# A hybrid decoder layer on one core: weights of the first projections by contraction block, and four edits to a planned order

## The chip, the cores and the metric

The kernel runs on one core of a Trainium2 chip. Its engines work side by side, each through its own list of instructions: TensorE (PE, with PEld for its weight loads), VectorE (DVE), ScalarE (ACT), GpSimd (POOL) and SyncE (SP), which issues nearly all transfers. The metric is the device time in microseconds (us) of one execution. Before the change the median of three runs is 917.85 us (917.58 to 918.46).

## The reference

One inference step of one layer, all in float32: a prompt of 512 tokens and 8 sequences of 4 new tokens each (544 tokens together, 1024 features).

```python
shift, scale, gate = jnp.split(jax.nn.silu(c) @ w_cond + b_cond, 3, axis=-1)
h = x * (1 + scale[:, None]) + shift[:, None]
qa, ka, va, za, qkv_b, zb, a_b, b_b, ga, gb = split_columns(h @ w_in)
# branch A: dilated sliding-window softmax attention, windows 128, 512, 2048, 8 heads x 64 each,
#           the three outputs combined by softmax-denominator share, times silu(za)
# branch B: conv of width 4 + silu on q/k/v, l2-normed q/k, chunked gated delta rule (8 heads x 128):
u = solve_unit_lower(I + strict(beta * k k^T * decay), [beta * v, beta * k * exp(cum)])
merged = sigmoid(ga) * (yA @ w_branch_a) + sigmoid(gb) * (yB @ w_branch_b)
y = LayerNorm(ALPHA * x + gate * (merged @ w_out))
```

(The line with `solve_unit_lower` stands for the triangular solve of each chunk of the delta rule.) It returns `y` for both kinds of tokens, the new key and value caches, and the states of branch B.

## The kernel before, in words

**Exact products in three passes.** TensorE multiplies float32 rounded to a shorter format (float32r) in one pass. Where full precision is wanted the kernel splits both operands into a rounded part and a rest (`hi`/`lo` of a weight, `hhi`/`hlo` of the activations) and sums `hhi*hi`, `hhi*lo` and `hlo*hi`. ACT makes `hi`, and DVE `lo`. Products in plain float32 (attention, delta rule) show as two records per matmul in the trace.

**The front.** `c` (`cT`, nine conditioning vectors, padded to 32 columns) is loaded on ACT's queue and gives `cs`, its silu. SP loads, in this order, eight 1 MB blocks `wm` of the conditioning weights; among them the constants `cst`, the activations `xT` in four loads of two blocks, and the first three weight tiles (128x1024, 512 KB each, into the three `wraw` buffers). For each of the eight contraction blocks k: eight matmuls make `pd` from `wm[k]` and `cs`; ACT copies it to `Y`; two small matmuls `pd<-cst,Y` turn it into scale and shift; DVE modulates `xT[k]`; ACT and DVE split it into `hhi`/`hlo`; and the first three projections (q, k and v of head 0 of branch B, jobs 0 to 2) take their three passes over block k. The weights of the first two are split in halves (`whi`, `wlo`, 128x512) and that of the third whole (`hi`, `lo`). They accumulate in the tiles `pp`, `pg` and `pb`. Fillers (`warm`) are put into TensorE's list where the planner expects it idle.

**The stream.** Some 90 more weight tiles (`wt<-in_w_in`) follow through the same three buffers, loaded by SP up to five jobs ahead and split up to two jobs ahead. Beside them run generators ("threads", each with a rank): the gates of branch B (`pg<-cg,abT` is the product that ends them), the inverses of the delta rule's chunks (`delta_blocks`, one thread for the eight heads, rank 1), the rule itself (rank 0), the attention of prompt and samples. In `delta_blocks` small blocks go through memory and back (`dtz` and `Tc`, `drows` and `cr`).

**The attention's probability products.** `prompt_attention` makes, for each of 4 head pairs and 4 query blocks, two transposed tiles `PT` of probabilities and then six or eight 128x64 by 128x128 matmuls `pg<-PT,vrow`, 120 in all.

**The end.** After the branches are merged (`mhi`, `mlo`, and `ms` for the sample rows), the last product runs over two halves of `w_out`: `wo0h`/`wo0l`, and then `wo1h`/`wo1l`. `load_out(n)` loads and splits a half in four pieces; DVE makes `r` and `lo` of an accumulator `pp` with the gate (`gs` of the samples, `gp` of the prompt), which frees it.

**The planner.** No engine's order is written by hand. Each call is recorded, and `schedule()` then places all instructions with a model of their costs: an instruction becomes a candidate once its inputs and a buffer are there by the model, and the candidate of the lowest rank and oldest number goes first on its engine. Calls inside `rec.together()` are placed without anything between them. `ENTER` is the model's cost of going over to another tile shape on TensorE, `op.extra` what a transfer takes beside its bytes until its reader may start, and `LINES` names the kinds of buffers that are given out per thread. The model only sets the order; on the chip each engine waits for what it needs. All instructions are emitted by one line, so in the profile every row of this kernel has L721 (after the change L722).

Of the kernel before, what the change touches and what calls it, by code (L numbers as in the profile page):

```python
# [259 lines left out]
class Recorder:  # L260
# [5 lines left out]
    AGAIN = {"pe": 0.0, "ve": 0.11, "se": 0.14, "ge": 0.11, "sp": 0.0}  # L266
    HOLD = 1.0
    GAP, HEAT, FULL = 0.25, 3.0, 17.0
    ENTER = {(128, 128): 0.197, (64, 128): 0.197, (64, 64): 0.142, (32, 32): 0.073, (128, 64): 0.1, (128, 32): 0.0,
             (64, 32): 0.1, (32, 128): 0.2, (32, 64): 0.1}  # L270
    ENGINES = ("pe", "ve", "se", "ge", "sp")
    FREE = ("g", "d", "b")

    def __init__(self):
        self.ops, self.events, self.rank, self.now, self.idle = [], [], 0, 0.0, 0.0
# [87 lines left out]
    def cost(self, op, args):  # L363
# [35 lines left out]
        elif e == "se":  # L399
            c = (0.155 if in_psum else 0.21) + 0.83e-3 * n  # L400
            a = (0.07 if "accum_out" in op.kw else 0.0) + (0.08 if pointer else 0.0)
            ix = op.outs[0].ix
            if n > 16 and ix.ndim > 1 and abs(int(ix.flat[1]) - int(ix.flat[0])) > 4:
                a += 1.0e-3 * n
            op.cost, op.late = c - 0.1 + a, 0.1
            f = args[2]
            op.table = None if f in (AF.Copy, AF.Square, AF.Abs) else "sqrt" if f == AF.Sqrt else "exp"
        elif e == "ge":
            c = {"memset": 0.08 + 0.85e-3 * n, "tensor_copy": 0.21 + 0.8e-3 * n,
                 "tensor_scalar": 0.25 + 2.45e-3 * n}.get(op.name, 0.25 + 2.05e-3 * n)  # L410
            op.cost, op.late = c - 0.05, 0.05
        else:
            runs, total = [], 0
            for v in (args[0], args[1]):
                r = 1
                if isinstance(v, View):
                    at = v.ix
                    steps = [(int(np.take(at, 1, axis=d).flat[0]) - int(at.flat[0]), k) if k > 1 else (0, 1)
                             for d, k in enumerate(at.shape)]
                    if v.base.pool.side != "dram":  # L420
                        steps = steps[1:]
                else:
                    steps = [(int(a), int(b)) for a, b in v.ap]
                for st, k in reversed(steps):
                    if k > 1 and st != r:
                        break
                    r *= k
                runs.append(min(r * 4, 32768))
            out = args[0]
            total = 4 * (out.ix.size if isinstance(out, View) else math.prod(b for _, b in out.ap))  # L430
            run = min(runs)
            dram = [not isinstance(v, View) or v.base.pool.side == "dram" for v in (args[0], args[1])]
            if not dram[0]:
                per, op.extra = run / (26e3 if self.front else 23.3e3), 1.75
                if isinstance(args[1], View):
                    op.extra += 1.0 if run >= 2048 else 2.3
            elif not dram[1]:
                per, op.extra = 0.026 + run / 60e3, 1.1
            else:
                per, op.extra = 0.044 + run / 21.7e3, 1.9  # L440
            if dram[0] and run < 512:
                op.extra += 0.5
            op.transfer = per * max(total / run / 16, 1)
            op.cost, op.late, op.table = 0.53 if dram[0] and dram[1] else 0.42, 0.0, None
            sbuf = [v for v in op.outs + op.ins if v.base.pool.side != "dram"]
            if sbuf and sbuf[0].shape[0] <= 32 and min(runs) < 2048:
                op.cost = 0.68


    def schedule(self):  # L450
# [9 lines left out]
        for op in ops:  # L460
# [6 lines left out]
            for t in op.tiles:  # L467
                if not hasattr(t, "left"):
                    t.left = 0
                    t.line = t.key + (op.part if t.kw.get("tag") in self.FREE else 0,)  # L470
                    tag.setdefault(t.key, []).append(t)
                    lines.setdefault(t.line, []).append(t)
                t.left += 1
# [300 lines left out]
def body(ctx, tc, io):  # L774
# [95 lines left out]
    ahead = {}  # L870
    with ExitStack() as fctx:
        fr = pool(fctx, "front", 1)
        cT = fr.tile([128, KT, 32], F32, name="cT")
        se.dma_start(cT, io["cT"])
        bT = fr.tile([128, 24], F32, name="bT")
        se.dma_start(bT, io["bT"])
        th = fr.tile([128, KT, 32], F32, name="th")
        se.activation(th, cT, AF.Tanh, scale=0.5)
        ve.tensor_scalar(th, th, 0.5, 0.5, op0=OP.mult, op1=OP.add)
        ve.tensor_mul(cs, cT, th)  # L880
        mb = fr.tile([128, KT, 2], F32, name="mb")
        ve.tensor_copy(mb[:, :, 0], bT[:, 0:8])
        ve.tensor_scalar(mb[:, :, 1], bT[:, 8:16], 1.0, None, op0=OP.add)
        xT = fr.tile([128, KT, NT], F32, name="xT")
        wm = [fr.tile([128, KT, 256], F32, name="wm", bufs=6) for _ in range(KT)]
        for k in range(KT):
            sp.dma_start(wm[k], io["w_mod"][k])
            if k == 0:
                sp.dma_start(cst, io["const"])
            if k % 2 == 0:  # L890
                sp.dma_start(xT[:, k:k + 2], io["xT"][:, k:k + 2])
            if k in FIRST:
                i = FIRST.index(k)
                raws[i] = wraw.tile([128, D], F32, name="wt", tag="wraw")
                sp.dma_start(raws[i], io["w_in"][TILE_AT["b", 0, (1, 0, 2)[i]]])
        rec.front = False
        sp.dma_start(wab, io["w_ab"])
        sp.dma_start(tables["g"], io["const_g"])
# [1 line left out]
        sp.dma_start(dta, io["dta"])  # L900

        for i in range(3):
            if i == 2:
                hi, lo = split(raws[i], D, ve)
                weights[i] = [(hi[:, 128 * k:128 * k + 128], lo[:, 128 * k:128 * k + 128]) for k in range(KT)]
                continue
            weights[i] = []
            for u in range(2):
                hi = op.tile([128, NT], F32R, name="whi", tag="o")[:, :512]
                lo = op.tile([128, NT], F32R, name="wlo", tag="o")[:, :512]  # L910
                raw = raws[i][:, 512 * u:512 * u + 512]
                se.activation(hi, raw, AF.Copy)
                ve.tensor_sub(lo, raw, hi.bitcast(F32))
                weights[i] += [(hi[:, 128 * k:128 * k + 128], lo[:, 128 * k:128 * k + 128]) for k in range(4)]
        ahead = {0: [pp(), pp()], 1: [pg(), pg()], 2: [pg(), pb_()]}
        mod = fr.tile([128, KT, 2, 9], F32, name="mod")
        xs = xT[:, :, SEQ:].rearrange("p k (b t) -> p k b t", t=4)
        for k in range(KT):
# [10 lines left out]
            pv = pc[:, 256:288].rearrange("p (a b) -> p a b", b=16)  # L929
            for u in range(2):  # L930
                pe.matmul(pv[:, u, 0:9], Y[:, 128 * u:128 * u + 128], C("selc"), start=True, stop=True)
            m = mod[:, k]
            ve.tensor_add(m, pv[:, :, 0:9], mb[:, k, :, None].to_broadcast([128, 2, 9]))
            per_token = lambda u: m[:, u, 1:9, None].to_broadcast([128, 8, 4])
            ve.tensor_mul(xs[:, k], xs[:, k], per_token(1))
            ve.tensor_add(xs[:, k], xs[:, k], per_token(0))
            h = xT[:, k]
            ve.tensor_scalar(h[:, :SEQ], h[:, :SEQ], m[:, 1, 0:1], m[:, 0, 0:1], op0=OP.mult, op1=OP.add)
# [522 lines left out]
    def prompt_attention():  # L1461

        for j in range(4):
# [55 lines left out]
            for i in range(4):  # L1519
# [12 lines left out]
                    PTs.append(PT)  # L1532
                    yield 1.2 + 0.5 * hh

                for c in range(c0_, 4):
                    for hh in range(2):
                        hp = slice(64 * hh, 64 * hh + 64)
                        g = max(c - 1, 0)
                        v = vrow[g][:, i - 1 if c == 0 else i, hp]
                        pe.matmul(pnv[hp, c > 1, i % 2, :], v, PTs[hh][:, c, :], start=c in (c0_, 2), stop=c in (1, 3))  # L1540
# [752 lines left out]
def lay_out(x):  # L2293
# [17 lines left out]
        "cT": np.pad(c.T.reshape(KT, 128, 9).transpose(1, 0, 2), ((0, 0), (0, 0), (0, 23))),  # L2311
# [18 lines left out]
        "ln_g": a["ln_g"],  # L2330
        "ln_b": a["ln_b"],
        "w_ab": w[:, OFF_AB:OFF_AB + 16].reshape(KT, 128, 16).transpose(1, 0, 2),
        "w_in": wt.reshape(len(TILES), KT, 128, 128).transpose(0, 2, 1, 3).reshape(len(TILES), 128, D),
    }
    return {k: np.ascontiguousarray(v) for k, v in d.items()}
# [34 lines left out]
```

## Time and profile before

| | |
|---|---|
| median of three runs | 917.85 us (917.58 to 918.46) |
| the profiled execution | 918.74 us |
| its span, first to last instruction | 917.0 us |
| mean granted clock of TensorE | 0.993 |
| TensorE busy | 893.8 us |
| DVE busy | 728.4 us |
| ACT busy | 430.3 us |
| moved by DMA | 239.50 MB, mean 261 GB/s |

Rows of the timeline read: start in us, duration in us, engine, line, operation, output<-inputs, shapes, count, and in brackets how long the engine had been idle and for what. A matmul's duration includes the way through the array, so matmuls that follow one another start closer together than they last, and the distance between starts is their price. Rows of groups show busy time and the mean of one in ns.

### The profile page before, as it was taken

The numbers are of one execution on the slowest core, as the hardware profiler recorded it, in microseconds if no ns is written. First come the engines' busy times: TensorE is split into PE (matmuls) and PEld (weight loads), VectorE is DVE, ScalarE is ACT, GpSimd is POOL, SyncE is SP. The second block draws the span as 40 slices with busy tenths as digits, with TensorE's granted clock in tenths as the row PEclk, the third lists the DMA queues.
The fourth block names the chain that finished last, engine by engine and source line by source line (L and its number), as shares of the span: only waits on it lengthen the run. The fifth ranks groups of instructions, "written<-read, shape, count | busy, mean of one in ns | idle before, by whom it ended". The sixth has DMA issues, their size and how long they took to land.

```text
span 917.0 us, 20414 instructions
## 1 busy us (share of the span) xinstructions
PE 893.8 (97%) x7874; PEld 835.8 (91%) x7874; DVE 728.4 (79%) x1637; ACT 430.3 (47%) x1007; POOL 77.4 (8%) x185
## 2 busy tenths in 40 slices
PE   8999999999999999999999999999999999999895
PEld 7899999899999999989899999999999999997684
DVE  3576757778568999989999987468879999867658
ACT  3375644867354675446657337524422222235311
POOL 0132011102000012001140000000110000000000
PEclk9999999999999999999999999999999999999998
DMA  9775777457758988989687785599899999988813
GB/s 372 287 196 196 223 215 237 143 174 239 231 171 274 301 278 281 297 260 333 214 299 238 255 258 161 173 298 378 261 335 362 324 398 418 335 308 299 266 41 118
DMA packets 108918, 239.50 MB, mean 261 GB/s; under 512 B 31554, under 2 KB 65484, under 8 KB 105108
## 3 DMA queue, kind: packets, MB, share of 16 engines
q1 hardware_dynamic: 108532, 238.04, 77.2%
q8 instruction: 62, 1.02, 0.5%
q14 instruction: 36, 0.29, 0.1%
q10 hardware_dynamic: 288, 0.14, 0.1%
HBM read 221.57 MB, written 104.26 MB: 355 GB/s over the span
## 4 chain that ended last, share of the span: by engine, by line
PE 79%; DVE 8%; DMA 6%; ACT 3%; SPq 1%; issue 1%; DVEq 0%; POOL 0%; ACTq 0%
PE pp L721 59%; PE pg L721 10%; PE pd L721 7%; PE pb L721 3%; DVE r L721 2%; DMA wm<-in_w_mod 2%; DVE acc L721 1%; SPq L721 1%; DMA rbo<-dO 1%; DMA wt<-in_w_in 1%; DVE lo L721 1%; DMA wv<-dw 1%; ACT L721 1%; DMA S<-in_state_delta 1%; DMA cT<-in_cT 1%
## 5 line engine op out<-in xcount | busy, mean ns | idle before, releaser
L721 PE MATMUL pp<-hhi,hi 128*128 128x272 f32 x1360 | 400.4, 294 | 2.7 <-DVE spare L721 1.8
L721 PE MATMUL pp<-hhi,lo 128*128 128x272 f32 x1360 | 400.6, 295 | 0.0
L721 PE MATMUL pp<-hlo,hi 128*128 128x272 f32 x1360 | 400.3, 294 | 0.0
L721 PEld LDWEIGHTS pp<-hhi,hi 128*128 128x128 f32 x1360 | 257.2, 189 | 5.4 <-DVE spare L721 2.1
L721 PEld LDWEIGHTS pp<-hlo,hi 128*128 128x128 f32 x1360 | 257.2, 189 | 2.9 <-issue 2.1
L721 PEld LDWEIGHTS pp<-hhi,lo 128*128 128x128 f32 x1360 | 256.8, 189 | 2.6 <-issue 1.6
L721 ACT ACTIVATE hi<-wt 128x1024 fp32r<-128x1024 f32 (+1 forms) x102 | 104.6, 1025 | 174.8 <-PE pp L721 141.5
L721 DVE TENSOR_TENSOR lo<-wt,hi 128x1024 fp32r<-128x1024 f32 (+1 forms) x102 | 120.1, 1177 | 40.6 <-ACT hi L721 40.1
L721 DVE SCALAR_TENSOR_TENSOR acc<-ext,cw,acc 128x568 f32<-128x568 f32 x72 | 57.4, 801 | 5.7 <-ACT acc L721 5.3
L721 ACT ACT_TABLE_LOAD x36 | 46.2, 1283 | 7.3 <-DVE acc L721 4.3
L721 DVE TENSOR_TENSOR slab<-slab 128x512 f32<-128x512 f32 (+1 forms) x66 | 43.0, 667 | 1.2 <-ACT slab L721 1.1
L721 DVE TENSOR_REDUCE slab<-slab 128x8 f32<-128x512 f32 (+2 forms) x66 | 43.0, 657 | 0.2
L721 POOL COPY cx<-ext 128x3 f32<-128x3 f32 (+1 forms) x48 | 33.9, 734 | 90.2 <-ACT ext L721 90.0
L721 ACT ACTIVATE zt<-pp 128x272 f32<-128x272 f32 x48 | 18.6, 388 | 45.8 <-PE pp L721 37.7
L721 ACT ACTIVATE P<-P,st 128x256 f32<-128x256 f32 (+1 forms) x64 | 31.2, 489 | 16.1 <-DVE st L721 15.7
L721 PE MATMUL pp<-ybl,hi 128*128 128x272 f32 x128 | 36.9, 289 | 0.0
L721 PE MATMUL pp<-ybh,hi 128*128 128x272 f32 x128 | 36.8, 288 | 0.0
L721 PE MATMUL pp<-ybh,lo 128*128 128x272 f32 x128 | 36.8, 287 | 0.0
L721 PE MATMUL pg<-k,q 128*128 128x128 f32 (+1 forms) x192 | 35.7, 308 | 0.4 <-DVE PT L721 0.3
L721 ACT ACTIVATE q<-pp 64x272 f32<-64x272 f32 (+1 forms) x48 | 26.3, 547 | 13.7 <-PE pp L721 13.2
L721 PEld LDWEIGHTS pg<-k,q 128*128 128x128 f32 x192 | 27.7, 191 | 3.3 <-issue 1.4
L721 DVE TENSOR_TENSOR Tb<-Tb,tmp 32x15 f32<-32x15 f32 (+7 forms) x120 | 23.4, 195 | 4.1
(405 smaller groups left out, 1635.0 us busy)
## 6 DMA issues: line engine op xcount, KB each, us to landing
out_kv_s<-in_cache SPq DMA_DIRECT2D x144, 512.0 KB
wt<-in_w_in SPq DMA_DIRECT2D x88, 512.0 KB
out_kv_s<-in_cache SPq DMA_DIRECT2D x24, 496.0 KB
wm<-in_w_mod SPq DMA_DIRECT2D x8, 1024.0 KB
slab<-in_ks SPq DMA_DIRECT2D x32, 256.0 KB
slab<-in_vs SPq DMA_DIRECT2D x32, 256.0 KB
kv<-in_ks SPq DMA_DIRECT2D x16, 512.0 KB
kv<-in_vs SPq DMA_DIRECT2D x16, 512.0 KB
```

The source lines that it names most:

```text
L721: getattr(real[x.engine], x.name)(*map(arg, x.args), **{k: arg(v) for k, v in x.kw.items()})
```

## The change

It has five edits; the computation stays as it is.

1. *Front.* The first three weights come as a new input `w_first`: for each contraction block a 128x384 slice of all three (192 KB, eight loads `wf` in four buffers), split block by block (`whi` on ACT, `wlo` on DVE). The `wraw` buffers are not used by them any more. `cT` is not padded: 9 columns, loaded by SP; `cs` is cleared and its first 9 columns are filled. `xT` comes in eight loads of one block. The split of blocks 0 and 7 into `hhi`/`hlo` is made in two halves of tokens, and the prompt's modulation stands ahead of the samples'.
2. *Products.* The probability products of one pair and query block stand in `rec.together()`.
3. *Inverses.* `delta_blocks` runs as two threads, one for the even heads and one for the odd (ranks 1 and 1.5). Buffers of kind `vr` are given out per thread.
4. *End.* The splits of the second half of `w_out` get rank 12.
5. *Model.* `ENTER` of 128x64 is 0.22 (was 0.1), and a value read back from memory is expected 1.9 us earlier (rows under 2048 bytes) or 0.4 us earlier (longer rows).

```diff
-    ENTER = {(128, 128): 0.197, (64, 128): 0.197, (64, 64): 0.142, (32, 32): 0.073, (128, 64): 0.1, (128, 32): 0.0,
+    ENTER = {(128, 128): 0.197, (64, 128): 0.197, (64, 64): 0.142, (32, 32): 0.073, (128, 64): 0.22, (128, 32): 0.0,
...
+    LINES = FREE + ("vr",)
...
-                    op.extra += 1.0 if run >= 2048 else 2.3
+                    op.extra += 0.6 if run >= 2048 else 0.4
...
-                    t.line = t.key + (op.part if t.kw.get("tag") in self.FREE else 0,)
+                    t.line = t.key + (op.part if t.kw.get("tag") in self.LINES else 0,)
...
-        cT = fr.tile([128, KT, 32], F32, name="cT")
-        se.dma_start(cT, io["cT"])
+        cT = fr.tile([128, KT, 9], F32, name="cT")
+        sp.dma_start(cT, io["cT"])
...
+        ve.memset(cs, 0.0)
...
-        ve.tensor_mul(cs, cT, th)
+        ve.tensor_mul(cs[:, :, 0:9], cT, th)
...
-            if k % 2 == 0:
-                sp.dma_start(xT[:, k:k + 2], io["xT"][:, k:k + 2])
-            if k in FIRST:
-                i = FIRST.index(k)
-                raws[i] = wraw.tile([128, D], F32, name="wt", tag="wraw")
-                sp.dma_start(raws[i], io["w_in"][TILE_AT["b", 0, (1, 0, 2)[i]]])
+            sp.dma_start(xT[:, k:k + 1], io["xT"][:, k:k + 1])
+            wf[k] = fr.tile([128, 384], F32, name="wf", bufs=4)
+            sp.dma_start(wf[k], io["w_first"][k])
...
+            whi = fr.tile([128, 384], F32R, name="whi", bufs=4)
+            wlo = fr.tile([128, 384], F32R, name="wlo", bufs=4)
+            se.activation(whi, wf[k], AF.Copy)
+            ve.tensor_sub(wlo, wf[k], whi.bitcast(F32))
...
-            se.activation(hhi[:, k, :], h, AF.Copy)
-            ve.tensor_sub(hlo[:, k, :], h, hhi[:, k, :].bitcast(F32))
+            for n in range(2) if k in (0, 7) else [0]:
+                w = slice(n * HF, (n + 1) * HF) if k in (0, 7) else slice(0, NT)
+                se.activation(hhi[:, k, w], h[:, w], AF.Copy)
+                ve.tensor_sub(hlo[:, k, w], h[:, w], hhi[:, k, w].bitcast(F32))
...
+                with rec.together():
+                    for c in range(c0_, 4):
...
-    blocks = threads.add(chain(delta_blocks, 8), 1)
+    for u in range(2):
+        threads.add(chain(lambda p, u=u: delta_blocks(2 * p + u), 4), 1 + 0.5 * u)
...
+            was, rec.rank = rec.rank, 12 if n else rec.rank
             se.activation(wo[n][0][:, k:k + 2], raw, AF.Copy)
             ve.tensor_sub(wo[n][1][:, k:k + 2], raw, wo[n][0][:, k:k + 2].bitcast(F32))
+            rec.rank = was
```

As the `wraw` buffers are free from the start, the planner puts a tile of the stream first on SP. SP's first rows before (DMA, output<-input, partitions x elements per partition):

```order
L721 DMA wm<-in_w_mod 128x2048
L721 DMA cst<-in_const 128x330
L721 DMA xT<-in_xT 128x1088
L721 DMA wm<-in_w_mod 128x2048
L721 DMA wt<-in_w_in 128x1024
L721 DMA wm<-in_w_mod 128x2048
```

and SP's first rows now:

```order
L722 DMA wt<-in_w_in 128x1024
L722 DMA cT<-in_cT 128x72
L722 DMA wm<-in_w_mod 128x2048
L722 DMA cst<-in_const 128x330
L722 DMA xT<-in_xT 128x544
L722 DMA wf<-in_w_first 128x384
```

The stream's tile and `cT` now stand ahead of the first `wm`, and slices `wf` follow where whole tiles stood.

On TensorE, in the middle of the prompt's attention, the probability products stood apart before (here two and five of eight, the missing one further up among the projections' matmuls):

```order
L721 MATMUL pg<-PT,vrow 64x128 x2
L721 MATMUL pb<-cst,KQ 128x128 x4
L721 MATMUL pg<-cst,P 128x128
L721 MATMUL pg<-k,q_574 128x128
L721 MATMUL pg<-k,q_588 128x128
L721 MATMUL pd<-U,NTs 64x64 x4
L721 MATMUL pg<-PT,vrow 64x128 x5
```

and now stand in one piece:

```order
L722 MATMUL pg<-k,q_645 128x128
L722 MATMUL pd<-Tc,NTs 32x16 x16
L722 MATMUL pg<-PT,vrow 64x128 x8
L722 MATMUL pd<-W_2197,Xc 32x16 x16
L722 MATMUL pg<-k,q_651 128x128
```

So the 120 products stand in 16 runs of six or eight instead of 32 runs of one to eight.

On DVE at the start of the last product, the splits of the second half (`wo1l`) stood ahead of the two operations that free the samples' accumulator (`r` and `lo` with `gs`):

```order
L721 TENSOR_TENSOR ms<-zt,ms 128x32
L721 MEMSET eps_11398 128x1
L721 TENSOR_TENSOR wo1l<-wo,wo1h 128x1024 x3
L721 SCALAR_TENSOR_TENSOR r_11431<-pp,gs 32x512
L721 SCALAR_TENSOR_TENSOR lo_11433<-pp,gs 32x512
L721 SCALAR_TENSOR_TENSOR r_11435<-pp,gp 128x512
```

and now:

```order
L722 TENSOR_TENSOR ms<-zt,ms 128x32
L722 MEMSET eps_11419 128x1
L722 TENSOR_TENSOR wo1l<-wo,wo1h 128x1024
L722 SCALAR_TENSOR_TENSOR r_11438<-pp,gs 32x512
L722 SCALAR_TENSOR_TENSOR lo_11445<-pp,gs 32x512
L722 TENSOR_TENSOR wo1l<-wo,wo1h 128x1024 x2
L722 SCALAR_TENSOR_TENSOR r_11463<-pp,gp 128x512
```

Two of the three splits have moved behind `r` and `lo`.

More of the change, by code (lines that the diff above doesn't have):

```diff
@@ L872, in body @@
         fr = pool(fctx, "front", 1)
-        cT = fr.tile([128, KT, 32], F32, name="cT")
-        se.dma_start(cT, io["cT"])
+        cT = fr.tile([128, KT, 9], F32, name="cT")
+        sp.dma_start(cT, io["cT"])
         bT = fr.tile([128, 24], F32, name="bT")
         se.dma_start(bT, io["bT"])
-        th = fr.tile([128, KT, 32], F32, name="th")
+        th = fr.tile([128, KT, 9], F32, name="th")
+        ve.memset(cs, 0.0)
         se.activation(th, cT, AF.Tanh, scale=0.5)
         ve.tensor_scalar(th, th, 0.5, 0.5, op0=OP.mult, op1=OP.add)
-        ve.tensor_mul(cs, cT, th)
+        ve.tensor_mul(cs[:, :, 0:9], cT, th)
         mb = fr.tile([128, KT, 2], F32, name="mb")
@@ L885, in body @@
         wm = [fr.tile([128, KT, 256], F32, name="wm", bufs=6) for _ in range(KT)]
+        wf = {}
         for k in range(KT):
@@ L902, in body @@
         for i in range(3):
[L903 to L914, printed above, removed]
+            raws[i], weights[i] = None, []
         ahead = {0: [pp(), pp()], 1: [pg(), pg()], 2: [pg(), pb_()]}
@@ L931, in body @@
                 pe.matmul(pv[:, u, 0:9], Y[:, 128 * u:128 * u + 128], C("selc"), start=True, stop=True)
+            whi = fr.tile([128, 384], F32R, name="whi", bufs=4)
+            wlo = fr.tile([128, 384], F32R, name="wlo", bufs=4)
+            se.activation(whi, wf[k], AF.Copy)
+            ve.tensor_sub(wlo, wf[k], whi.bitcast(F32))
+            for i in range(3):
+                weights[i].append((whi[:, 128 * i:128 * i + 128], wlo[:, 128 * i:128 * i + 128]))
             m = mod[:, k]
@@ L934, in body @@
             per_token = lambda u: m[:, u, 1:9, None].to_broadcast([128, 8, 4])
+            h = xT[:, k]
+            ve.tensor_scalar(h[:, :SEQ], h[:, :SEQ], m[:, 1, 0:1], m[:, 0, 0:1], op0=OP.mult, op1=OP.add)
             ve.tensor_mul(xs[:, k], xs[:, k], per_token(1))
             ve.tensor_add(xs[:, k], xs[:, k], per_token(0))
-            h = xT[:, k]
-            ve.tensor_scalar(h[:, :SEQ], h[:, :SEQ], m[:, 1, 0:1], m[:, 0, 0:1], op0=OP.mult, op1=OP.add)
-            se.activation(hhi[:, k, :], h, AF.Copy)
-            ve.tensor_sub(hlo[:, k, :], h, hhi[:, k, :].bitcast(F32))
+            for n in range(2) if k in (0, 7) else [0]:
+                w = slice(n * HF, (n + 1) * HF) if k in (0, 7) else slice(0, NT)
+                se.activation(hhi[:, k, w], h[:, w], AF.Copy)
+                ve.tensor_sub(hlo[:, k, w], h[:, w], hhi[:, k, w].bitcast(F32))
             rec.rank = 9
@@ L1533, in prompt_attention @@
                     yield 1.2 + 0.5 * hh
[L1535 to L1540, printed above, removed]
+                with rec.together():
+                    for c in range(c0_, 4):
+                        for hh in range(2):
+                            hp = slice(64 * hh, 64 * hh + 64)
+                            g = max(c - 1, 0)
+                            v = vrow[g][:, i - 1 if c == 0 else i, hp]
+                            pe.matmul(pnv[hp, c > 1, i % 2, :], v, PTs[hh][:, c, :], start=c in (c0_, 2), stop=c in (1, 3))
                 if i % 2:
@@ L2310, in lay_out @@
         "xT": rows.T.reshape(KT, 128, NT).transpose(1, 0, 2),
-        "cT": np.pad(c.T.reshape(KT, 128, 9).transpose(1, 0, 2), ((0, 0), (0, 0), (0, 23))),
+        "cT": c.T.reshape(KT, 128, 9).transpose(1, 0, 2),
         "w_cond": a["w_cond"][0][:, 2 * D:],
@@ L2332, in lay_out @@
         "w_ab": w[:, OFF_AB:OFF_AB + 16].reshape(KT, 128, 16).transpose(1, 0, 2),
+        "w_first": wt[[TILE_AT["b", 0, s] for s in (1, 0, 2)]].reshape(3, KT, 128, 128).transpose(1, 2, 0, 3).reshape(KT, 128, 384),
         "w_in": wt.reshape(len(TILES), KT, 128, 128).transpose(0, 2, 1, 3).reshape(len(TILES), 128, D),
```

## Prediction

> **What bounds the kernel now.** I read the page first: the span, the busy shares, the 40 slices, the chain.
>
> ```profile
> span 917.0 us, 20414 instructions
> PE 893.8 (97%) x7874; PEld 835.8 (91%) x7874; DVE 728.4 (79%) x1637; ACT 430.3 (47%) x1007; POOL 77.4 (8%) x185
> PE   8999999999999999999999999999999999999895
> PE 79%; DVE 8%; DMA 6%; ACT 3%; SPq 1%; issue 1%; DVEq 0%; POOL 0%; ACTq 0%
> ```
>
> TensorE is busy 97% of the span, and only the first slice and two of the last three (of 22.9 us each) show less than nine tenths. So between some 50 and 850 us time is gained only by taking work off TensorE, and at the two ends by taking away what it waits for. The list of its waits says how little waiting there is to remove.
>
> ```profile
> PE pp L721 <- DVE lo L721: 2.1, 1, 2.1
> PE pp L721 <- DVE spare L721: 1.8, 1, 1.8
> PE pd L721 <- DVE XF L721: 1.4, 2, 0.9
> PE pd L721 <- DVE cs L721: 1.3, 1, 1.3
> ```
>
> The columns are total us, times, longest. Span less busy time is 23.2 us in all. One wait, 2.1 us for DVE's `lo`, is the largest.
>
> Then the front, by its two windows (span from:to, length, busy time of PE, PEld, DVE, ACT, POOL, clock, DMA share, GB/s), and one piece of the chain.
>
> ```profile
> 7.66:34.66 27.00, 25.84 (x253) 20.31 (x254) 13.53 (x36) 9.62 (x18) 0.00 (x0) 1.00 1.02 413
> 34.66:48.42 13.76, 13.76 (x118) 12.54 (x118) 8.18 (x19) 6.32 (x15) 6.29 (x17) 1.00 0.55 178
> 16.77 17.75 DMA wm<-in_w_mod
> 34.66 1.07 PE L721 MATMUL pd<-wm,cs 128*32 128x256 f32 x16 [0.17 <-DMA wm<-in_w_mod]
> ```
>
> Until 34.66 us the DMA engines are full (share 1.02, 413 GB/s) and the chain runs through the `wm` transfers: the last conditioning product starts when the last `wm` lands. After it TensorE is busy without a gap. So the front has two parts: one as long as its bytes, one as long as the matmuls left over behind the last `wm`.
>
> **The change part by part: front.** The bytes ahead of the last `wm` stay the same. The three first projections' 1.5 MB now come as eight 192 KB slices instead of three whole tiles, and one 0.5 MB stream tile that came among the later `wm` loads now comes first. So I leave the arrival at 34.7 us. What changes is what TensorE can do before it: in program order 99 matmuls stand between the last conditioning product and the gate product (`pg<-cg,abT`) before, 83 now. The third projection needs its split block by block now, and joins the other two in step.
>
> ```profile
> 39.36 0.29 PE L721 MATMUL pb<-hhi,hi 128*128 128x272 f32 x1
> 39.49 0.28 PE L721 MATMUL pg<-hhi,lo 128*128 128x272 f32 x1
> 48.42 0.61 PE L721 MATMUL pg<-cg,abT 32*128 32x16 f32 x4
> 35.86 0.37 ACT L721 ACTIVATE Y<-pd 128x256 f32<-128x256 f32 x1
> 36.12 0.65 ACT L721 ACTIVATE hhi<-xT 128x544 fp32r<-128x544 f32 x1
> 38.09 1.06 ACT L721 ACTIVATE hi<-wt 128x1024 fp32r<-128x1024 f32 x1 [1.32 <-DMA wt<-in_w_in]
> ```
>
> Such matmuls start 0.13 us apart (39.49 less 39.36), and 16 of them are 2.0 us. That is the term: **-2.0 us**. The room for them ahead of 34.66 us comes from fillers (24 now, 29 before) and from the idle 1.16 us of the first window (27.00 less 25.84). Against it stands ACT's queue: the last split of a `wf` slice (384 columns, between `Y`'s 0.37 for 256 and `hhi`'s 0.65 for 544, so about 0.5) now stands ahead of the last `Y`, and two `hi` of 1.06 stand ahead of the two halves of the last `hhi`. From 35.7 on I get `Y` at 36.5, its product and the modulation to about 38.0, the halves of `hhi` ready at 38.6 and 40.0; TensorE has 33 matmuls (4.1 us) in front of the first matmul that reads the last block, and reaches it at 39.9. That is hidden, by a margin of about 1 us for the first half and none for the second. Bounds: 0 (transfers or ACT eat it) and -4 (a part of the idle time at the start goes too).
>
> The unpadded `cT` moves from ACT's queue to SP's, behind one 0.5 MB load; the `cs` wait of 1.3 us is ahead of a stretch that ends with the last transfer, so I put it at nothing; without that cover, 0.5 MB at 413 GB/s are 1.2 us more.
>
> [...]
>
> **Probability products.** `PT,vrow` has 120 matmuls (each two records). Before, the order has them in 32 groups of one to eight, now in 16 of six or eight. The price of a group and of a change of kind:
>
> ```profile
> 159.97 0.88 PE L721 MATMUL pg<-PT,vrow 128*64 128x128 f32 x12
> 160.78 0.49 PE L721 MATMUL pg<-k,q 128*128 128x128 f32 x2
> 170.34 0.37 PE L721 MATMUL pp<-hlo,hi 128*128 128x272 f32 x1
> 170.64 0.43 PE L721 MATMUL pg<-PT,vrow 128*64 128x128 f32 x2
> 171.00 0.39 PE L721 MATMUL pp<-hhi,lo 128*128 128x272 f32 x1
> 171.24 0.29 PE L721 MATMUL pp<-hhi,hi 128*128 128x272 f32 x1
> ```
>
> Six products together last 0.81 us (160.78 less 159.97), one alone 0.36 (171.00 less 170.64). So one more costs 0.09 and a group 0.27 beside its products. Sixteen groups less are -4.3 us. Entering from a projection matmul takes 0.30 (170.64 less 170.34) against the usual 0.13, so 0.17 more; about half of the lost groups stand behind such a matmul: 8 x 0.17 = -1.4. Against it, the new order breaks other runs: it has five more groups of 128x32 products (0.17 each, +0.9), and goes 16 times more between the projections' matmuls and the others, 8 returns at 0.11 each (171.24 less 171.00, less 0.13), +0.9. Sum **-3.9 us**; bounds -2 (only the groups, half of them paid for elsewhere) and -6. Nothing hides this: TensorE is the bound there.
>
> **Tail.** Second half of `wo`: its splits get rank 12, that is, they give way to other work on ACT and DVE.
>
> ```profile
> 856.96 3.50 DVE L721 TENSOR_TENSOR wo1l<-wo,wo1h 128x1024 fp32r<-128x1024 f32 x3 [1.17 <-ACT wo1h L721]
> 861.06 0.68 DVE L721 SCALAR_TENSOR_TENSOR lo<-pp,gs 32x512 f32<-32x512 f32 x1
> 861.89 0.47 PE L721 MATMUL pp<-wo0h,mhi 128*128 128x512 f32 x1 [2.06 <-DVE lo L721]
> 863.41 0.63 PE L721 MATMUL pp<-wo0h,mlo 128*128 128x512 f32 x1
> 863.84 0.63 PE L721 MATMUL pp<-wo0h,mhi 128*128 128x512 f32 x1
> 866.32 0.39 PE L721 MATMUL pp<-wo0h,mhi 128*128 128x512 f32 x1
> 866.55 0.39 PE L721 MATMUL pp<-wo0l,mhi 128*128 128x512 f32 x1
> 859.40:862.80 3.40, 1.34 (x6) 0.80 (x5) 3.35 (x5) 1.18 (x2) 0.00 (x0) 1.00 0.85 273
> 862.80:866.20 3.40, 3.40 (x10) 2.62 (x9) 3.40 (x6) 1.06 (x1) 0.00 (x0) 0.50 0.71 259
> ```
>
> Before, `r` and `lo`, which free the accumulator, queue behind three `wo1l` (3.50 us); in the new order they stand behind one. One takes 1.17, so `lo` ends about 2.3 us earlier and the wait of 2.06 us goes: -2.0. The low-busy stretch (PE 1.34 of 3.40) is followed by one at half the granted clock, where matmuls start 0.43 apart (863.84 less 863.41) instead of 0.23 (866.55 less 866.32). Eight matmuls at 0.20 more are 1.6; I take -1.5 for a clock that stays up. Sum **-3.5 us**, bounds -1 (the two late `wo1l` are waited for at the start of the second half) and -4.
>
> [...]
>
> **Shorter allowances and two chains.** The planner now expects values read back from memory 1.9 us earlier (short rows: `Tc`, `Ls`) or 0.4 us earlier (long rows), and the eight heads' inverses are two threads instead of one. Neither changes an instruction's duration. Both change who stands where.
>
> ```profile
> 270.57 0.43 SPq L721 DMA_DIRECT2D Tc<-dtz  x1
> 274.59 0.30 DVE L721 STREAM_TRANSPOSE Xc<-Tc 128x128 f32<-128x128 f32 x1
> 516.73 0.38 SPq L721 DMA_DIRECT2D Tc<-dtz  x1
> 523.67 0.31 DVE L721 STREAM_TRANSPOSE Xc<-Tc 128x128 f32<-128x128 f32 x1
> DVE NTs L721 <- DMA cr<-drows: 1.3, 1, 1.3
> ```
>
> The readers start 4.0 and 6.9 us after the issue and never waited; readers that stand 1.9 us nearer would wait only where there was less slack than that. If DVE waits, its next operations wait too (splits `lo` first, which feed the stream of projections two jobs ahead), and TensorE only after these. I take **+1.5 us**: one wait as long as the one of `cr` shown, reaching TensorE. Bounds 0 and +5 (three or four such). The two more table loads on ACT lie on an engine that is 47% busy: nothing.
>
> **Sum.** -2.0 - 3.9 - 3.5 + 1.5 = -7.9. The profiled execution took 918.7 us for a span of 917.0, which makes 910.8; the median of three runs is 0.9 below the profiled one, so **909.9 us**.
>
> **Rivals.** (A) *The front stays as long*: the last slice or the last `hhi` is late. For: SP's eight `wf` are each the last transfer of their block, and the margin of the second half is nothing. Against: 4.1 us of other matmuls. Without the 2.0: 911.9. (B) *The tail's wait moves* to `wo1l`, or the low clock stays: for, the two delayed splits must still be done before the second half; against, the half starts several microseconds later. Without the 3.5: 913.4. (C) *More stalls go*: two chains give TensorE other work when one inverse waits; the waits for `XF` and `spare` (3.2 us), and the 1.5 I charge, go: 905.2. (D) *Slower: the read-backs wait.* Eight heads with two short read-backs each, 1.9 us nearer, are 30 us of possible waits on DVE, which is busy 79% and has little room to catch up. If half of them reach TensorE through late splits, that is 15 us in place of the 1.5: 923.4. It decides from 9.4 us of waits on TensorE (7.9 and the 1.5 already charged). For: every head has them, so the waits would repeat. Against: the slack of 4.0 and 6.9 us in the rows above, and projections that TensorE has ready. (E) *The new order's drift cancels the gain*: the whole order stands otherwise after a change at the start, and waits of the size of those listed come back several times over: 917.9. [...]
>
> **How the numbers follow.** Forecast 0.45, own range 905.5 to 914 (the five uncertainties of about 2 us each, added as squares). A 0.13, B 0.12, C 0.13, D 0.08, E 0.06, F 0.03. What a measurement of this kernel tells from no change is about 0.2%, 1.8 us. Faster, below 916.0: forecast, A, B, C and a little of E, 0.85. Within: most of E, 0.05. Slower: D, F, the rest, 0.10. The range, 903.5 to 916.5, leaves out D, F, most of E and the ends of C.
>
> **What would show it.** Front: the gate product at about 46.4 instead of 48.4, no wait for `whi` or `hhi`. Products: `PT,vrow` in 16 groups, each 0.81 or about 1.0 us. Tail: no wait for `lo`, clock 1.00 in the stretch after it, `wo1l` x1 and then x2. Wrong would be: TensorE waits for `Xc`, `XF`, `rb` or `QKd` of more than 3 us in sum, idle time in the front behind 34.7, or a second stretch of half clock.

## The result, and the profile after

The changed kernel takes 911.92 us (median of four runs, 910.69 to 912.24) against 918.15 us of the kernel before on the same chip (four runs, 917.58 to 918.88). The ratio is 0.9929, with a 95% interval of 0.9912 to 0.9946: 6.2 us faster. The profiled execution took 912.15 us for a span of 910.4. Its page, the same rows as before:

```profile
span 910.4 us, 20432 instructions
PE 887.0 (97%) x7864; PEld 831.7 (91%) x7864; DVE 729.0 (80%) x1643; ACT 434.7 (48%) x1014; POOL 70.7 (8%) x185
PE   9999999999999999999999999998999999999995
PE 67%; DVE 13%; DMA 10%; ACT 5%; issue 2%; SPq 2%; POOL 0%; DVEq 0%; ACTq 0%
```

TensorE's first slice is full now and the dip near the end is gone. Its share of the chain that ended last fell from 79% to 67%; DVE and DMA took its place, although TensorE's busy share is 97% as before. That is a first hint that something was lost between the ends.

Three places, in rows of the timeline of the changed kernel (the front, and DVE at the start of the last product):

```profile
34.44 1.07 PE L722 MATMUL pd<-wm,cs 128*32 128x256 f32 x16 [0.34 <-DMA wm<-in_w_mod]
36.48 0.36 ACT L722 ACTIVATE Y<-pd 128x256 f32<-128x256 f32 x1
38.52 0.41 ACT L722 ACTIVATE hhi<-xT 128x272 fp32r<-128x272 f32 x1
39.83 0.41 ACT L722 ACTIVATE hhi<-xT 128x272 fp32r<-128x272 f32 x1
46.37 0.61 PE L722 MATMUL pg<-cg,abT 32*128 32x16 f32 x4
854.28 1.23 DVE L722 TENSOR_TENSOR wo1l<-wo,wo1h 128x1024 fp32r<-128x1024 f32 x1 [1.17 <-ACT wo1h L722]
856.11 0.68 DVE L722 SCALAR_TENSOR_TENSOR lo<-pp,gs 32x512 f32<-32x512 f32 x1
856.82 2.36 DVE L722 TENSOR_TENSOR wo1l<-wo,wo1h 128x1024 fp32r<-128x1024 f32 x2
```

The last `wm` lands 0.2 us earlier than before (34.44 instead of 34.66) and the gate product stands at 46.37 instead of 48.42. `lo` runs between the splits `wo1l`, and no wait for it is left.

The span cut at the gate product and at the first long run of the last product gives the balance. First the kernel before, then the changed one (columns as in the prediction: from:to, length, busy time of PE and so on):

```profile
48.42:853.53 805.11, 797.76 (x7225) 755.76 (x7224) 659.81 (x1494) 398.92 (x950) 70.88 (x165) 1.00 0.81 268
853.53:917.00 63.47, 51.09 (x258) 42.08 (x258) 45.88 (x84) 13.79 (x22) 0.00 (x0) 0.92 0.37 125
```

```profile
46.37:850.85 804.48, 793.50 (x7224) 753.58 (x7223) 661.11 (x1497) 403.14 (x953) 66.18 (x166) 1.00 0.81 268
850.85:910.40 59.55, 49.30 (x258) 40.93 (x258) 45.86 (x84) 13.88 (x22) 0.00 (x0) 0.95 0.38 132
```

Front -2.05 us, tail -3.92, and the 800 us between only -0.63. Yet in those the probability products alone became shorter, from 20.2 to 15.5 us (from a run's first start to the next start behind it, summed over 32 and 16 runs). And the kernel before had a stretch at half clock there:

```profile
50.43:53.84 3.41, 2.48 (x25) 2.16 (x25) 2.93 (x8) 3.32 (x10) 1.23 (x6) 1.00 0.94 100
53.84:57.25 3.41, 3.41 (x17) 3.41 (x16) 3.12 (x8) 1.53 (x10) 0.79 (x2) 0.50 0.95 214
```

TensorE did half of a window's work in it, 1.7 us lost, and the changed kernel's profile has none: its clock is 1.00 from 6.26 to 903.97 us. 4.7 and 1.7 are 6.4 us less, of which 0.63 arrived: something took back 5.8 us, in part as idle time of TensorE: 7.35 us there before (805.11 less 797.76), 10.98 now. TensorE's steps from a matmul of the projections (into `pp`) to one of another kind, waits included, sum to 48.8 us before and 52.6 now, from the gate product to the first product with `w_out`. The question for the experiments is where that comes from.

### The profile page after: what moved, and what is told of

The parts are those of the page before. It is cut to its first block, busy times and chain, and to the rows that moved or that the text cites. A ratio compares the mean times of both kernels' runs of the same rounds, so it can differ in the third digit from the quotient of the medians.

```text
span 910.4 us, 20432 instructions
## 1 busy us (share of the span) xinstructions
PE 887.0 (97%) x7864; PEld 831.7 (91%) x7864; DVE 729.0 (80%) x1643; ACT 434.7 (48%) x1014; POOL 70.7 (8%) x185
## 4 chain that ended last, share of the span: by engine, by line
PE 67%; DVE 13%; DMA 10%; ACT 5%; issue 2%; SPq 2%; POOL 0%; DVEq 0%; ACTq 0%
PE pp L722 51%; PE pg L722 8%; PE pd L722 6%; PE pb L722 3%; DVE r L722 2%; SPq L722 2%; DMA wt<-in_w_in 2%; DVE acc L722 1%; ACT L722 1%; DMA rbo<-dO 1%; DVE slab L722 1%; DMA xT<-in_xT 1%; DVE lo L722 1%; DMA dk<-pair 1%; DMA wf<-in_w_first 1%
## 5 line engine op out<-in xcount | busy, mean ns | idle before, releaser
L722 ACT ACT_TABLE_LOAD x38 | 48.8, 1283 | 5.5 <-DVE acc L722 3.7
L722 POOL COPY cx<-ext 128x3 f32<-128x3 f32 (+1 forms) x48 | 25.9, 570 | 66.2 <-ACT ext L722 66.1
L722 DVE CUSTOM_DVE_ANT_0 P<-pg,bias 128x256 f32<-128x256 f32 (+1 forms) x64 | 24.3, 402 | 5.9 <-PE pg L722 5.4
```

The source lines that it names most:

```text
L722: getattr(real[x.engine], x.name)(*map(arg, x.args), **{k: arg(v) for k, v in x.kw.items()})
```

## The experiments

Every run was compared with the kernel before on its own chip.

| run | edits on | ratio | 95% interval |
|---|---|---|---|
| e1 | rank 12 | 0.9962 | 0.9949 to 0.9975 |
| e2 | products together | 0.9982 | 0.9968 to 0.9997 |
| e3 | front | 0.9918 | 0.9904 to 0.9932 |
| e4 | none; 4 ns in the model | 1.0032 | 1.0015 to 1.0048 |
| e5 | front, rank 12 | 0.9896 | 0.9879 to 0.9914 |
| e6 | all but together | 1.0048 | 1.0030 to 1.0066 |
| e7 | all but allowances | 0.9910 | 0.9890 to 0.9930 |
| e8 | all but two chains | 0.9946 | 0.9930 to 0.9962 |
| e9 | front, rank 12, together | 0.9902 | 0.9886 to 0.9918 |
| e10 | all (again) | 0.9954 | 0.9938 to 0.9970 |
| e11 | all but `ENTER` | 0.9884 | 0.9864 to 0.9905 |
| e12 | all but together and `ENTER` | 1.0049 | 1.0031 to 1.0067 |

The theory at the start: the three gains named in the prediction (front, products, tail) are real where they stand, and the middle's is lost to the planner's new order. Its rivals: one of the edits costs it, above all the shorter allowances.

**e1, the tail alone.**

```diff
+            was, rec.rank = rec.rank, 12 if n else rec.rank
...
+            rec.rank = was
```

> The kernel before with one edit: the splits of the second half of w_out get rank 12. TensorE's list stays the same, DVE's and ACT's change only in the last 60 us. Theory (wait and clock go together): the wait for lo of 2.06 us goes, and with it the half-clock stretch behind it, 1.6 to 1.9 us; from the first wo0h product to the end 59.6 us instead of 63.5, the run 3.9 us faster, about 914.2. Rival (the granted clock does not hang on this wait): only the wait goes, the stretch at 0.50 stays somewhere in the tail, 2.0 us faster, 916.1. Rival (the late wo1l are waited for): under 1 us.

Measured 914.35 us, ratio 0.9962: 3.5 us faster (2.3 to 4.7). The profile's tail, and the middle ahead of it:

```profile
48.54:851.82 803.28, 796.52 (x7225) 754.43 (x7224) 660.15 (x1495) 399.15 (x950) 72.20 (x166) 1.00 0.81 269
851.82:911.40 59.58, 49.33 (x258) 40.93 (x258) 45.87 (x84) 13.88 (x22) 0.00 (x0) 0.95 0.39 134
```

59.58 us instead of 63.47: the theory's number. But the middle, in which TensorE's list is that of the kernel before, is 1.83 us shorter too, and this profile has no half-clock stretch at 54 us (mean clock from 48 to 140 us 1.00, 0.98 in the kernel before). So that stretch belongs to a single execution, not to the order, and the one in the tail may, too. Against this profile of the same order the changed kernel's middle is not shorter at all (804.48).

**e2, the products alone.**

```diff
+                with rec.together():
```

> The kernel before with one edit: the probability products of one pair and query block stay together. Theory: 16 runs of products instead of 32, together 15.5 us instead of 20.2 on TensorE, and the order's drift on top: 2 to 6 us faster, 912 to 916. Rival (the planner's new order gives it back through more changes of kind and new waits): within 1.5 us of before, 916.6 to 919.6, though the products themselves are 4.7 us shorter.

916.06 us, ratio 0.9982: 1.6 us faster (0.3 to 2.9). Neither number of the expectation is excluded; the theory's lower end and the rival meet. The products' group fell from 22.4 to 16.6 us of busy time (the 16 runs are 15.5 us as in the changed kernel), and new waits of TensorE stand in the list:

```profile
PE pb L721 <- DVE crow L721: 1.5, 1, 1.5
PE pb L721 <- ACT QKd L721: 1.4, 1, 1.4
PE pg L721 <- ACT PT L721: 1.0, 1, 1.0
```

None of the three is among the waits of 0.3 us or more in the kernel before. The steps from a projection's matmul to another kind sum to 56.2 us instead of 48.8. Most of the 4.7 us came back.

**e3, the front alone**, with the front's part of the diff (`cT`, `cs`, `xT`, `wf`, `whi`/`wlo`, halves of blocks 0 and 7).

> The kernel before with the front's edits alone (w_first slices, cT unpadded, xT by block, halves of blocks 0 and 7). Theory: the last wm lands at 34.4 to 34.7 us as before, 83 matmuls instead of 99 lie behind it, the gate product at 46.4 instead of 48.4: 2.0 us faster from there, with drift of 2 us either way behind it: 914 to 918. Rival (the half-clock stretch of 53.84 to 57.25 us hangs on the front's end): another 1.7 us, the granted clock 1.00 until 60 us. Rival (nothing but drift is gained): gate product at 48.

910.33 us, ratio 0.9918: 7.5 us faster (6.2 to 8.8), by the medians more than the whole change, though the intervals overlap. The gate product stands at 46.35, so 2.07 us are the front's own. The rest came behind it: from there to the last product's first long run 799.2 us (46.35 to 845.52) against 803.3 in e1, the same work in another order. The tail says something on the clock. It has the wait for `lo` still, cut here into windows of 3.41 us, the length of the half-clock stretch of the kernel before; where they begin is my estimate:

```profile
853.88 0.47 PE L721 MATMUL pp<-wo0h,mhi 128*128 128x512 f32 x1 [2.04 <-DVE lo L721]
```

```profile
848.73:852.15 3.42, 3.10 (x14) 2.17 (x12) 3.20 (x3) 2.09 (x3) 0.00 (x0) 1.00 0.81 274
852.15:855.56 3.41, 1.68 (x7) 1.43 (x8) 3.37 (x6) 1.27 (x3) 0.00 (x0) 1.00 1.12 413
855.56:858.97 3.41, 3.41 (x16) 2.77 (x15) 3.00 (x5) 0.97 (x1) 0.00 (x0) 1.00 0.80 237
```

The same wait of 2.0 us, and the clock stays at 1.00: the wait falls into two windows, and neither is emptier than 1.68 of 3.41.

**e4, a probe of the order as such.**

```diff
-    WAKE = {"pe": 0.06,
+    WAKE = {"pe": 0.064,
```

> The kernel before with one number of the planner's model moved by 4 ns (the time TensorE takes to see a signal, 0.060 to 0.064 us). No work is added, removed or changed; the planner only breaks some ties otherwise and TensorE's order differs in the middle. Theory (the middle of the changed kernel lost 4 us to a new order as such): the span between the gate product and the first wo0h product moves by 1 to 4 us, up or down, with no wait above 2 us to blame. Rival (the order as such is worth nothing, the loss has a cause in the edits): within 0.7 us of before.

920.85 us, ratio 1.0032: 2.9 us slower (1.4 to 4.4), from 4 ns in a number of the planner's model. The expectation's "no wait above 2 us to blame" is not met in full: one wait for `spare` grew from 1.8 to 2.2 us in the profile, and a half-clock stretch follows it (mean clock from 480 to 640 us 0.99, 1.00 in the kernel before). Its profiled execution took 918.84 us, 2.0 less than the median, so the profile does not show where all of the 2.9 us lie. It is one such probe: it shows that an order alone can be worth about 3 us, and not how far orders scatter.

**e5, front and tail.**

> The kernel before with two edits: the front and rank 12 for the late splits. TensorE's list is that of the front alone, so only the last 60 us can differ from it. Theory (the two gains are in different places and add): the front alone stands at 0.9918 of before and the rank alone at 0.9962, together 0.988, about 906.3, and faster than the whole change (0.9929), since the middle keeps the order that the front alone gave. Rival (the front alone had already gained the tail's clock by its phase, so only the wait of 2.0 us is left): 0.9895. Rival (the gain of the front alone was luck of the chip session): 0.992 or more.

908.17 us, ratio 0.9896: the first rival's number (0.9895) and not the sum (0.988), though the interval holds both. Against e3 the tail is worth 2.0 us here by the ratios, whose intervals overlap, and 2.3 in the profiles (61.8 and 59.5 us from the last product's first long run to the end): the wait, and no half-clock stretch (mean clock 0.96 from 846.36 us on, where the kernel before has 0.92 from 853.53 on). Alone in e1 it was 3.5. This version, without the products' edit, the chains and the model's numbers, is faster than the whole change (0.9929, and 0.9954 in e10).

**e6, e7 and e8: the change with one part undone** (the reverse of `rec.together()`, of the allowances, and of the two threads).

> The changed kernel without the edit that keeps the probability products together (43 runs of them in the order instead of 16). Theory (the products' 4.7 us come back as later starts behind projections, as they did when this edit was made alone): within 2 us of the changed kernel, ratio to before 0.991 to 0.995, though the products take 20 to 22 us instead of 15.5. Rival (the prediction's: a gain of some 4 us of their own): 0.997 or more. Rival (it does harm in company): 0.990 or less.

921.77 us, ratio 1.0048. Both my theory and the harm in company are out; it lost even more than the prediction's rival said. It is 9 to 11 us slower than the change. The products are in 43 runs, 23.1 us instead of 15.5, and 7.6 us would be the larger part of that; e12 below tests it. The wait for `spare` is 3.3 us and followed by a half-clock stretch (mean clock from 560 to 640 us 0.98), and in its profile the last `wm` product starts at 36.66 us, 2.2 late.

> The changed kernel with the old, longer allowances for values read back from memory. Theory of the prediction (the shorter ones cost about 1.5 us of waits): ratio about 0.991. Rival (they are the cause of the 4 us that the middle lost): 0.9885 or less. Rival (no cause, only another order): anywhere within 0.990 to 0.996, with waits for read-backs as in the changed kernel.

909.51 us, ratio 0.9910, the number of the prediction's theory: 1.7 us better than the change in its first measurement, 4.0 better than in e10's, with intervals that overlap in the first case and lie just apart in the second. But the waits do not tell this theory from the last rival. DVE's waits for four kinds of values read back (`cr`, `rb`, `wv`, `Tc`), in the kernel before, in the changed kernel, and in e7 (total us, times, longest):

```profile
DVE NTs L721 <- DMA cr<-drows: 1.3, 1, 1.3
DVE QKd L721 <- DMA rb<-dr: 1.1, 1, 1.1
DVE ya L721 <- DMA wv<-dw: 0.3, 1, 0.3
DVE NB L721 <- DMA wv<-dw: 0.2, 1, 0.2
```

```profile
DVE ya L722 <- DMA wv<-dw: 2.2, 1, 2.2
DVE NTs L722 <- DMA cr<-drows: 2.1, 2, 1.2
DVE QKd L722 <- DMA rb<-dr: 1.5, 2, 1.1
DVE Xc L722 <- DMA Tc<-dtz: 1.4, 1, 1.4
```

```profile
DVE Xc L722 <- DMA Tc<-dtz: 2.9, 2, 2.7
DVE ya L722 <- DMA wv<-dw: 1.5, 1, 1.5
DVE NB L722 <- DMA wv<-dw: 1.4, 1, 1.4
DVE NTs L722 <- DMA cr<-drows: 1.2, 1, 1.2
```

2.9, 7.2 and 7.0 us: with the long allowance DVE waits as long as in the changed kernel, and for `Tc` longer (2.9 instead of 1.4). Over all profiles these waits are 2.9 to 7.0 us with the long allowance and 3.5 to 7.2 with the short one. That is the rival "no cause, only another order", with its number (0.990 to 0.996) met as well; that the allowances cost 1.5 us is not shown.

> The changed kernel with one thread for the eight heads' inverses, as before. Theory: the two threads gain or lose no more than the order's drift, ratio 0.990 to 0.996. Rival (two threads shorten the waits for XF and for the attention): 0.996 or more, with more waits for XF. Rival (the second thread takes TensorE and DVE from the stream of projections): 0.9885 or less.

912.76 us, ratio 0.9946, between the change's two measurements (0.9929 and 0.9954): the two threads are worth nothing that can be told.

**e9, the products in a third company** (front, rank 12, together).

> The kernel before with three edits: front, rank 12, and products kept together (16 runs). Its difference to front and rank alone (0.9896) is the products' edit in a third company. Theory (the 16 runs are 15.5 us instead of 20.6, and the order's drift of 3 us either way comes on top): ratio 0.982 to 0.990. Rival (late starts behind projections give it back, as when it was made alone): 0.988 to 0.992, with the steps from a projection matmul to another kind some 5 us longer in sum. Rival (best of all): below 0.984.

908.16 us, ratio 0.9902 against e5's 0.9896: the rival, though the theory's upper end lies inside the interval. The runs are 15.5 us instead of 20.6, and the time does not move. TensorE's steps from a projection's matmul to one of another kind sum to 51.2 us where e5 has 47.7, 3.5 and not 5 us longer, and some waits are longer. The first row of this kernel's list (0.9 in e5), and the one for `spare` (0.4 in e5):

```profile
PE pg L721 <- DMA rbo<-dO: 2.1, 1, 2.1
PE pp L721 <- DVE spare L721: 1.3, 1, 1.3
```

Its profile also has half clock in the front (0.50 from 9.17 to 12.58 us), whose first `wm` came 1.9 us late; the mean clock of the whole is 0.992, e5's 0.997.

**e10, the change again.**

> The changed kernel once more, on the chip of the runs beside it. Theory: 0.9929 within 0.002; a second profile shows what belongs to the order (waits at the same places) and what to the single execution: where the last wm lands (35.1 us in the first profile) may move by 1 to 2 us, and a half-clock stretch may turn up or not. Rival: a profile that repeats the first within 0.3 us everywhere, so that the half-clock stretches of before belong to its order.

912.47 us against 916.71, ratio 0.9954. That is 0.0025 from the first measurement, more than I expected; the changed kernel differs by 0.55 us between the two chips and the kernel before by 1.4. Taken together the change is worth 4 to 6 us. Its profile repeats the first: gate product 46.36, middle 803.95 instead of 804.48 at a clock of 1.00 in both, tail 59.49 instead of 59.55. So the middle's loss belongs to the order and not to one execution.

**e11, the old cost of entering.**

```diff
-    ENTER = {(128, 128): 0.197, (64, 128): 0.197, (64, 64): 0.142, (32, 32): 0.073, (128, 64): 0.22, (128, 32): 0.0,
+    ENTER = {(128, 128): 0.197, (64, 128): 0.197, (64, 64): 0.142, (32, 32): 0.073, (128, 64): 0.1, (128, 32): 0.0,
```

> The changed kernel with the old cost of entering 128x64 in the planner's model (0.1). The products stand in 16 runs either way. Theory (a number of the model alone): within the order's drift of 3 us, ratio 0.990 to 0.996. Rival (the new number is what lost the middle its gain): 0.989 or less.

906.76 us, ratio 0.9884: the rival. The change without this number is 6.4 us faster than the change in e10, measured beside it (0.9954 less 0.9884), with intervals that do not meet, and the fastest kernel measured, with e5 inside its interval. Page and list of waits of this kernel:

```profile
span 902.6 us, 20407 instructions
PE 883.2 (98%) x7864; PEld 830.8 (92%) x7864; DVE 729.1 (81%) x1643; ACT 430.1 (48%) x1010; POOL 71.2 (8%) x185
```

```profile
PE pp L722 <- ACT ext L722: 1.7, 3, 0.9
PE pd L722 <- DMA wm<-in_w_mod: 1.7, 2, 1.4
```

There is no wait for `spare` (1.1 and 1.3 in the change's two profiles). TensorE's busy time is 4.5 us less than e10's 887.7 and its idle time 19.4 us instead of 22.1. The products stand in 16 runs of the same 15.5 us in both, so the number didn't act on what it prices; it gave the planner another order. Whether it would in another kernel, or is chance as with the 4 ns of e4, these runs don't tell; in e6's company, as e12 shows next, the same number is worth nothing.

**e12, without the products' edit and that number.**

> The changed kernel without the products' edit and without the new entering cost: 31 runs of products in the order, where the change without the products' edit alone has 43 (and 1.0048 of before). Theory (each run of products costs 0.27 us wherever it stands, and 43 runs were the larger part of that loss): 12 runs less are 3.2 us less, the ratio 0.997 to 1.002. Rival (the loss lay elsewhere, in waits): 1.004 or more. Rival (with the new number away the products' edit is worth nothing): 0.993.

921.16 us, ratio 1.0049: the rival, the loss lay elsewhere. The products are 19.7 us now, 3.4 less than in e6, and the time is the same. The profile names the largest wait. TensorE, DVE at that place, and TensorE's windows around it:

```profile
621.77 0.60 PE L722 MATMUL pp<-hhi,hi 128*128 128x272 f32 x1 [4.74 <-DVE spare L722]
611.87 1.05 DVE L722 TENSOR_TENSOR ya<-ya,wv 128x512 f32<-128x512 f32 x1 [2.05 <-DMA wv<-dw]
619.22 1.02 DVE L722 TENSOR_TENSOR NB<-NB,wv 128x512 f32<-128x512 f32 x1 [0.45 <-DMA wv<-dw]
620.15 1.21 DVE L722 TENSOR_TENSOR lo<-wt,hi 128x1024 fp32r<-128x1024 f32 x1
621.28 0.43 DVE L722 SCALAR_TENSOR_TENSOR spare<-spare,pp 128x272 f32<-128x272 f32 x1
```

```profile
616.24:619.66 3.42, 0.79 (x7) 0.57 (x5) 2.98 (x5) 0.40 (x1) 0.00 (x0) 1.00 1.14 300
619.66:623.07 3.41, 1.30 (x6) 1.30 (x6) 3.41 (x6) 0.00 (x0) 1.29 (x3) 0.50 1.15 387
623.07:626.49 3.42, 3.42 (x17) 3.42 (x17) 2.55 (x6) 0.63 (x1) 0.18 (x1) 0.50 1.03 335
```

At the end of the prompt's attention DVE combines the parts of the heads' outputs (`ya` and `NB`). It waits 2 us for `wv`, which comes back from memory, and the rest of its list slides behind that: more of `ya` and `NB`, an update of the samples' state, a split, and only then `spare<-spare,pp`, which frees the accumulator that the next projection needs. TensorE stands 4.74 us, a window has 0.79 us of work, and the next two run at half the clock. In the second of these TensorE is busy throughout and does half, 1.7 us lost. As with `lo` in the tail, the operation that frees an accumulator stands late in DVE's list; there it stood behind three splits, and no read from memory. In the fourteen profiles the wait for `spare` is anything from nothing (e2, e11) to 4.74 us. The order is most of that; the kernel before and e1, with one list of TensorE, differ by 0.6 (1.8 and 1.2).

## Why the prediction was right, and where not

The time, 911.92, is 2.0 above the 909.9 forecast and inside its range; faster was given 0.85. The front and the tail came as reasoned, the products' term did not. How near the gain came to the forecast is in part luck: it was 6.2 us here and 4.2 in e10, where the kernel before took 1.4 us less. Point by point:

- **Front, -2.0 us: right**, 2.05. 16 matmuls fewer behind the last `wm`, at 0.13 us; that is 2.1, of which 1.83 show behind the last `wm` (13.76 us to the gate product before, 11.93 now), and the last `wm` product stands 0.22 earlier. The halves of the last `hhi` end at 38.93 and 40.24 us, 0.3 and 0.2 behind the 38.6 and 40.0 at which they were to be ready, and TensorE waits for neither. The stretch of the transfers is as long as before, so rival F, that the smaller transfers run slower, falls: eight slices of 192 KB and the halved `xT` loads among other transfers cost nothing here (416 GB/s from 7.48 to 34.44 us instead of 413 from 7.66 to 34.66, the last `wm` product at 34.44 instead of 34.66). The loads ahead of the first `wm`, put at nothing, are not always free: of the ten profiles with this front seven have the gate product at 46.3 to 46.6 us, and e7, e6 and e9, in which TensorE waits 1.0, 2.6 and 1.9 us for the first `wm`, at 47.6, 48.5 and 49.4. The four with the old front have it at 48.4 to 48.8. SP issues that load at 1.64 us in the changed kernel; why it lands later in these three stays open. (e11 waits 1.4 us for it and still has 46.6.)
- **Products: the price was right, the cover was wrong.** The runs were to be 4.3 us shorter, and are 4.7. But "nothing hides this: TensorE is the bound there" failed. Alone the edit gave 1.6 us, on top of front and tail nothing, and undone from the change it cost 9 to 11. The other changes of kind were to add up to 0.4 us (-1.4, 0.9 and 0.9); the steps out of the projections alone became 3.8 us longer (48.8 to 52.6), and 7.5 in e2. TensorE is busy 97% and still waits for DVE and ACT at a few places, and which of them wait, and how long, changes with each order by as much as the runs became shorter.
- **Tail, -3.5 us: right for the wait, half right for the clock.** 3.92 us in the profile. The wait's 2.0 us goes in every profile with this edit. The 1.5 to 1.9 for the clock was paid in the kernel before and in e2, and with the same wait not in e3 and e4 (mean clock from 840 us on 0.93 and 0.92, and 0.94 in both others; one half-clock stretch is 0.02 of these 80 us). The difference of e5 and e3 is 2.0 to 2.3, e1 gave 3.5.
- **Allowances, +1.5 us: not shown.** e7 is 1.7 to 4.0 us better without the shorter ones, about the 3 us that e4's order alone was worth, and DVE's waits for read-backs are as long with the old ones (7.0 us) as with the new (7.2). Rival D names the mechanism that was found at `spare`, but at one place, not in all heads.
- **`ENTER` was not priced at all.** With it the order is 6.4 us worse in the change's company, and no worse in e6's. The prediction folded the new order into "+1.5, one wait as long as the one of `cr`". The orders that these runs tried differ by more: 2.9 us for 4 ns in e4.
- **The sum** was -7.9 and the result -6.2 (-8.1 to -5.0), and -4.2 (-5.7 to -2.8) when measured again, which leaves the forecast's 7.9 out: front and tail gave 6.0 us where 5.5 were forecast, and the middle 0.6 instead of 2.4, though a half-clock stretch less helped it.
- Rivals: A and B fall by the front's and the tail's rows. E, the new order's drift, falls as a number (917.9), but it is what happened to the middle: 5.8 us. C, more stalls going, did not come true for the change. In e11 the wait for `spare` is gone and that for `XF` is not (1.1 us), and nothing shows that the two chains did it.

## What to carry to other kernels

When a planner sets the order, judge a local edit by the local rows (runs, waits, where a stage starts) and probe the order itself with an edit that means nothing. Here one such probe moved the time by 3 us, as much as each gain that was forecast, and one number of the model moved it by twice that in one company and not at all in another. Look for the operation that frees an accumulator late in an engine's list, behind splits (`lo`) or a read from memory (`spare`): TensorE stood 2 to 4.7 us there, and lost 1.7 more where the clock fell behind it. When a list of waits is compared between runs, sum all rows of the kind. And test the parts apart before keeping the whole: two of the edits (e5) gave more than all of them.

## What the runs showed of the hardware

In the kernel before the granted clock changes at 53.84, 57.25, 862.80, 866.21 and 910.59 us: 1, 236, 1 and 13 times 3.413 us apart. The first stretch on record starts at 6.05 us, 14 times 3.413 ahead of the first change; in the changed kernel it starts at 6.26 and the one change stands 263 times 3.413 behind that, at 903.97. The grid lies otherwise in each of the executions shown here: counted from the span's start these changes stand 2.6 and 2.9 us behind a whole number of such steps, and e12's at 619.66 us 1.9.

What went with a change was how busy TensorE was in one such window. In the profiles of the kernel before and of the changed one, from the first recorded step on, every window with TensorE busy 1.35 us or less was followed by one at half clock (the one at 859.4 us shown in the prediction, and the ends of both programs), and of the windows with 2.1 us or more only the one at 50.43 in the kernel before (2.48 us, shown above). Rows of other runs lie between and below: e12's windows with 0.79 and 1.30 us (above) were followed by half clock, e3's with 1.68 us was not. The two cases nearest to each other, from e9's front and e5's end:

```profile
5.76:9.17 3.41, 1.55 (x15) 1.28 (x18) 0.00 (x0) 0.00 (x0) 0.00 (x0) 1.00 1.00 376
9.17:12.58 3.41, 3.41 (x25) 2.44 (x18) 0.56 (x2) 0.80 (x2) 0.00 (x0) 0.50 1.02 410
```

```profile
894.05:897.46 3.41, 1.61 (x14) 1.40 (x12) 3.37 (x10) 0.30 (x1) 0.00 (x0) 1.00 0.04 14
897.46:900.88 3.42, 0.00 (x0) 0.00 (x0) 3.28 (x9) 0.29 (x1) 0.00 (x0) 1.00 0.40 153
```

1.55 us of work were followed by half clock, and 1.61 were not (where e5's windows begin is my estimate). If that holds in general, which these few rows don't show, a wait of 2.06 us with TensorE busy around it halves the clock when at least 1.86 of it (3.41 less 1.55) lie in one window. If the grid falls anywhere, that is (3.41 - 2.06 + 2 x 0.20)/3.41, by this estimate about half of the executions, and the wait's price is some 2.9 us on average (2.06 + 0.5 x 1.7). Of the four profiles with the wait for `lo`, two had the half-clock stretch. The planner's code asks for 1.65 us in a window; e5's 1.61, just below that, kept the clock. Why 2.48 us was not enough at 50.43 us, in one execution of the kernel before, stays open; those matmuls were of several kinds, and a record missing from the trace can't be excluded.
